# Seven products of quadrants instead of eight in the down projections of two squared-relu MLPs

## The chip, the cores and the metric

The kernel runs on one core of a Trainium2 chip. The metric is the device time of one execution in microseconds (us). The inputs are float32; 512 tokens, 1024 features.

## The reference, cut to what matters

A first block (attention mixers, gated MLP, embedding gate) is followed by two layers; each ends with a squared-relu MLP, between two RMS norms and with a residual:

```python
def squared_relu_mlp(h, w_up, w_down):        # h 512x1024, w_up 1024x4096, w_down 4096x1024
    u = jax.nn.relu(h @ w_up)
    return (u * u) @ w_down

        ff = squared_relu_mlp(rms_norm(h, mlp_norm_pre[layer]), mlp_w_up[layer], mlp_w_down[layer])
        h = h + rms_norm(ff, mlp_norm_post[layer])
```

## The kernel before

All activations lie feature-major: a tile holds 128 features (partitions) by 512 tokens. A product in float32 precision is made of three passes: each operand is split into a rounded high part (`hi`, a cast on ScalarE) and the rest (`lo`, a subtraction on VectorE), and `mm3` (line 404 for each matmul) adds hi·hi, hi·lo and lo·hi in PSUM. Weights come by DMA as 128x1024 tiles (`raw`, four buffers), and are split in `_split` into `whi` (L361, ScalarE) and `wlo` (L365, VectorE), four buffers each. `take` hands out one weight tile; it issues the splits up to three tiles ahead and the loads up to five tiles ahead, in the order that a dry run has recorded. Activations are split in `split_to` (L562 on ScalarE, L563 on VectorE).

The engines run their own queues. The framework that builds the program puts in the semaphores and lays out the order within each queue; the order of the source is its priority.

The working tiles of 128x512 float32 (2 KB a partition) come from 72 slots, taken and given back by `get` and `put`, oldest free first. PSUM has eight banks of 128x512, from `ps` and `pput`.

One MLP (`mlp`): `layer_start` computes the first five up tiles (four of them in two token halves) and the statistics of the norm. Each of 32 up tiles is 8 k tiles x 3 passes = 24 matmuls with the weights stationary and the 512 tokens moving. Its output gets a relu on VectorE (L1902), a Square on ScalarE (L1907) and the split. After 16 up tiles `half_down` multiplies them with the first K half of the down weights: 8 output tiles, each 16 k x 3 matmuls, copied to `ya` by ScalarE (L1585). After the other 16, `close` does the second K half: six output tiles whole, the last two (`tail = 2`) in two token halves of 256 columns, so that the norm (`rms_g`: column sums by matmul, a reciprocal root in small VectorE operations in `rsqrt`, a broadcast by two transposes, L588) and the residual (`postnorm`) of one token half run under the matmuls of the other. The second half's norm and residual (`fin`) run under the first matmuls of the next layer, or at the end of the kernel, where POOL and VectorE share the additions and the result is stored (L636).

After the first MLP, `xs` (the residual stream, 8 tiles) stays in its slots; `spill` and `fill`, which write it to DRAM and read it back, are used around the mixers only.

The value projections (`vals`) are token-major: there the activations are the stationary operand and 256 columns of weights move.

Of the kernel before, what the change touches and what calls it, by code (L numbers as in the profile page):

```python
# [19 lines left out]
P = 128  # L20
T = 512
# [1 line left out]
NT = T // P  # L23
EPS = 1e-6
BIGM = 1e30
NSLOT = 72
LOOK_SPLIT = 3
LOOK_DMA = 5
LO_CHUNK = 1024
# [32 lines left out]
NCOL = _n  # L62
NPAIR = 22
UP_ORDER = [m for i in range(NPAIR) for m in (i, i + NPAIR)]


def _bucket(rel):
# [56 lines left out]
    return np.ascontiguousarray(a.reshape(k // (nk * P), P, nk * n))  # L124


def _cv(v):
    return np.asarray(v).reshape(-1, P).T

# [6 lines left out]
def layout(I):  # L136
    I = {k: np.asarray(v) for k, v in I.items()}
    A = {}
    A["xt"] = np.ascontiguousarray(I["x"][0].T).reshape(8, P, T)
    A["pt"] = np.ascontiguousarray(I["p"][0, 0].T).reshape(2, P, T)  # L140
    A["pos"] = np.ascontiguousarray(I["positions"][0].reshape(NT, P).T)
    w = I["w_in"][0]
    sl = lambda a, n: w[:, a:a + n]
    q0, kv0, g0, cq0, ckv0, kr0, mg0 = 0, 512, 1280, 1304, 1560, 1688, 1720
    kv = [sl(kv0 + 128 * i, 128) for i in range(6)]
    A["win"] = _mtiles(np.concatenate(
        [kv[0], kv[1], kv[2], kv[4], sl(q0, 512), sl(cq0, 256), sl(ckv0, 128), sl(mg0, 2048)], 1))
# [24 lines left out]
    A["kvv"] = np.concatenate([_ktiles(wkv[:, 1024 + 256 * i:1280 + 256 * i], 4) for i in range(4)], 0)  # L172
    A["wq"] = _mtiles(I["b_w_q_2"][0])
    A["bwo"] = _mtiles(I["b_w_out_2"][0])
    for l in range(2):
        A[f"mup{l}"] = _mtiles(I["mlp_w_up_2"][l])
        A[f"mdn{l}"] = _mtiles(I["mlp_w_down_2"][l])
# [90 lines left out]
class Em:  # L268
    def __init__(self, nc, pools, A, order=None, dbg=None):
        self.nc, self.pools, self.A = nc, pools, A  # L270
        self.order, self.rec = order, []
        self.dry = order is None
        self.pos = self.dma_pos = self.spl_pos = 0
        self.raw, self.ready = {}, {}
        self.free = deque(range(NSLOT))
# [5 lines left out]
        self.fin = None  # L281
        self.closing = False
        self.peak = 0
        self.dbg = dbg or {}


    def get(self, name, dt=F32):
        i = self.free.popleft()
        self.peak = max(self.peak, NSLOT - len(self.free))
        if self.dry:  # L290
            t = _Null()
        else:
            t = self.pools["slots"].tile([P, T], dt, name=name, tag=f"sl{i}", bufs=1)
        self.slot_of[id(t)] = (i, t)
        return t

    def put(self, *ts):
        for t in ts:
            i, _ = self.slot_of.pop(id(t))
            self.free.append(i)  # L300

    def tile(self, pool, shape, dt, name, bufs=None):
        if self.dry:
# [22 lines left out]

    @staticmethod
    def width(key):
        return key[2] * key[4] * P if key[0] == "A" else key[3]

    def _dma(self, i):
        key = self.order[i]
        e = self.width(key)
        t = self.tile("raw", [P, 1024], F32, "raw")
        if key[0] == "A":
# [61 lines left out]
    def takeT(self, w, i, nk, n):  # L397
        hi, lo = self.take(("T", w, i, nk * n))
        f = lambda t: t.rearrange("p (k c) -> p k c", k=nk)
        return f(hi), f(lo)  # L400


# [311 lines left out]
    def finish(self, gen=()):  # L714


        for n, _ in enumerate(gen):
            if n + 1 in FIN and self.fin is not None:
                if next(self.fin, self) is self:
                    self.fin = None  # L720
        if self.fin is not None:
            drain(self.fin)
            self.fin = None

    @contextmanager
    def after(self, *ins):
# [140 lines left out]

def _emit(s):
    nc = s.nc
    V, S, G = nc.vector, nc.scalar, nc.gpsimd  # L870
    A = s.A

# [1002 lines left out]
    ho = [ho[i] for i in range(8)]  # L1875
    for i, (h, l) in enumerate(ho):
        s.dump("ho", h.bitcast(F32) if not s.dry else h, i)
    fill(xs)
    s.wlo = LO_ENG[3]
    ys, ss = [], s.get("ss")  # L1880
    (acts,) = s.close("awo", ho, 0, 4, s.yevac(ss, ys, "a_post"), ss, ys, xs, ["mlp_pre0"], pre)


    def mlp(l, acts, gains):


        first, banks, eps = layer_start(f"mup{l}", acts, True)
        yacc = []
        ss = s.get("ss")
        for half in range(2):  # L1890
            hid = []
            for m in range(16 * half, 16 * half + 16):
                if m < 5:
                    pieces = first[m]
                    ps = pieces[0][0]
# [12 lines left out]
                hid.append(s.split(t))  # L1908
                s.put(t)
            if half == 0:  # L1910
                half_down(f"mdn{l}", hid, 0, yacc)
        s.putacts(acts)
        return s.close(f"mdn{l}", hid, 16, 2, acc_evac(ss, yacc, f"mlp_post{l}"), ss, yacc, xs, gains, None, eps,
                       s.out if l else None)

    (qacts,) = mlp(0, acts, ["b_pre"])

# [167 lines left out]
    do = [do[i] for i in range(8)]  # L2085
    for i, (h, l) in enumerate(do):
        s.dump("do", h.bitcast(F32) if not s.dry else h, i)
    fill(xs)
    s.wlo = LO_ENG[5]
    ys, ss = [], s.get("ss")  # L2090
# [6 lines left out]
def tile_kernel(ctx, tc, A, out, dbg=None):  # L2097
# [15 lines left out]
    e2.out = out  # L2113
    e2.tc = tc
    _emit(e2)
# [14 lines left out]
```

## Time and profile before

| | |
|---|---|
| median of 3 runs | 2155.44 us (2153.95 to 2160.1) |
| the profiled execution | 2165.75 us, its span 2164.0 us |
| granted TensorE clock over the span | 0.984 |
| TensorE (PE) busy | 2118.6 us, 11650 matmuls |
| VectorE (DVE) busy | 1385.8 us, 2934 instructions |
| ScalarE (ACT) busy | 1041.9 us, 1966 instructions |
| moved by DMA | 222.58 MB, mean 103 GB/s |

The span goes from the first to the last instruction. The time of the execution lies a little above the span. PEld is TensorE's weight load, SPq the queue that issues the DMAs. The end of a matmul is modelled, since matmuls are pipelined; the distance from start to start tells what one costs.

### The profile page before, as it was taken

What the parts mean: (1) busy time and instruction counts of PE and PEld (TensorE: products, weight loads), DVE (VectorE), ACT (ScalarE), POOL (GpSimd) and SP (SyncE); (2) the same over time, 40 slices, a digit from 0 to 9 for tenths busy, and PEclk for the clock granted to TensorE, in tenths of its full rate; (3) what the DMA queues carried; (4) which work ended last, traced back from release to release, by engine and by line L of the source; (5) the groups of instructions that cost most, each with busy time, mean ns of one, the idle gap of its engine ahead of it and who ended that gap; (6) DMA issues with size and microseconds to landing.
All of it is one profiled execution on the core that took longest, in us unless ns stands there. A gap on an engine that the chain in (4) does not pass through costs nothing.

```text
span 2164.0 us, 30979 instructions
## 1 busy us (share of the span) xinstructions
PE 2118.6 (98%) x11650; PEld 1814.9 (84%) x11650; DVE 1385.8 (64%) x2934; ACT 1041.9 (48%) x1966; POOL 143.8 (7%) x264
## 2 busy tenths in 40 slices
PE   9999999999999999899999999999999999999997
PEld 8888877988888899789779888888988889888887
DVE  7686688787367578877997632444777758423443
ACT  5565576554344455555655432333456645323341
POOL 0000002000000000422430000000000000000001
PEclk9999999999999999899999999999999989999999
DMA  6113256332333333122121333224463531332331
GB/s 220 43 62 101 66 171 216 98 107 77 104 103 98 106 112 127 54 75 69 59 93 65 107 98 98 97 92 133 136 188 103 147 102 60 97 98 98 98 97 40
DMA packets 95125, 222.58 MB, mean 103 GB/s; under 512 B 9696, under 2 KB 32080, under 8 KB 94976
## 3 DMA queue, kind: packets, MB, share of 16 engines
q1 hardware_dynamic: 94976, 220.61, 32.1%
q8 instruction: 91, 1.49, 0.3%
q14 instruction: 58, 0.48, 0.1%
HBM read 198.25 MB, written 17.87 MB: 100 GB/s over the span
## 4 chain that ended last, share of the span: by engine, by line
PE 49%; DVE 4%; POOL 2%; issue 1%; ACT 1%; DMA 1%; POOLq 0%; SPq 0%; ACTq 0%; DVEq 0%
PE ps L404 47%; PE s L404 1%; PE o L404 1%; POOL lx L1759 1%; POOL lx L1758 1%; DMA dtab<-rexp 1%; PE rms L404 1%; DVE wlo L365 0%; DVE lx L1761 0%; PE rms L588 0%; DVE lx L1762 0%; DMA raw<-in_mup 0%; DVE sc L1787 0%; DVE ls L1669 0%; PE pt L829 0%
## 5 line engine op out<-in xcount | busy, mean ns | idle before, releaser
L404 PE MATMUL ps<-ah,whi 128*128 128x512 f32 (+1 forms) x2414 | 916.0, 380 | 1.7 <-ACT whi L361 1.1
L404 PE MATMUL ps<-ah,wlo 128*128 128x512 f32 (+1 forms) x2414 | 904.6, 375 | 0.0
L404 PE MATMUL ps<-al,whi 128*128 128x512 f32 (+1 forms) x2414 | 900.4, 373 | 1.9 <-DVE al L566 1.4
L361 ACT CAST whi<-raw 128x1024 fp32r<-128x1024 f32 (+4 forms) x323 | 316.4, 983 | 572.6 <-PE ps L404 545.3
L365 DVE TENSOR_TENSOR wlo<-raw,whi 128x1024 fp32r<-128x1024 f32 (+4 forms) x323 | 374.2, 1160 | 266.2 <-ACT whi L361 264.2
L404 PEld LDWEIGHTS ps<-ah,wlo 128*128 128x128 f32 x2414 | 454.3, 188 | 86.7
L404 PEld LDWEIGHTS ps<-al,whi 128*128 128x128 f32 x2414 | 455.0, 188 | 83.1 <-DVE al L566 2.3
L404 PEld LDWEIGHTS ps<-ah,whi 128*128 128x128 f32 x2414 | 455.2, 189 | 78.2 <-ACT whi L361 1.4
L1902 DVE TENSOR_SCALAR mu<-ps 128x512 f32<-128x512 f32 (+1 forms) x72 | 45.2, 632 | 149.6 <-PE ps L404 149.6
L404 PE MATMUL ps<-ah,wh 128*128 128x256 f32 x428 | 122.2, 285 | 0.0
L404 PE MATMUL ps<-al,wh 128*128 128x256 f32 x428 | 121.0, 283 | 0.0
L404 PE MATMUL ps<-ah,wl 128*128 128x256 f32 x428 | 121.0, 283 | 0.0
L797 ACT ACTIVATE p<-p,am 128x128 f32<-128x128 f32 (+3 forms) x160 | 88.5, 554 | 39.6 <-DVE am L795 38.6
L404 PE MATMUL ps<-whi,ah 128*128 128x256 f32 (+2 forms) x300 | 88.8, 296 | 3.9 <-DVE am L795 3.3
L404 PE MATMUL ps<-wlo,ah 128*128 128x256 f32 (+2 forms) x300 | 87.2, 291 | 0.9 <-DVE wlo L365 0.9
L621 DVE TENSOR_TENSOR ss<-ss,sq 128x512 f32<-128x512 f32 (+1 forms) x117 | 67.3, 575 | 31.5 <-ACT sq L620 30.5
L404 PE MATMUL ps<-whi,al 128*128 128x256 f32 (+2 forms) x300 | 87.1, 291 | 0.0
L404 PEld LDWEIGHTS ps<-al,wh 128*128 128x128 f32 x428 | 81.9, 191 | 0.3
L404 PEld LDWEIGHTS ps<-ah,wh 128*128 128x128 f32 x428 | 81.9, 191 | 0.2
L404 PEld LDWEIGHTS ps<-ah,wl 128*128 128x128 f32 x428 | 81.9, 191 | 0.0
L565 ACT ACTIVATE ah<-x,cols 128x256 fp32r<-128x256 f32 (+1 forms) x96 | 49.5, 540 | 52.8 <-DVE x L632 49.6
L835 ACT CAST pth<-pt 128x128 fp32r<-128x128 f32 (+3 forms) x128 | 49.9, 431 | 40.7 <-PE pt L829 38.3
(326 smaller groups left out, 2740.6 us busy)
## 6 DMA issues: line engine op xcount, KB each, us to landing
raw<-in_mup SPq DMA_DIRECT2D x64, 512.0 KB, 3.5
raw<-in_mdn SPq DMA_DIRECT2D x64, 512.0 KB, 3.8
raw<-in_up SPq DMA_DIRECT2D x44, 512.0 KB, 3.5
raw<-in_win SPq DMA_DIRECT2D x26, 512.0 KB, 3.9
raw<-in_awin SPq DMA_DIRECT2D x24, 512.0 KB, 3.5
thd<-th SPq DMA_DIRECT2D x24, 256.0 KB, 2.3
th<-thd SPq DMA_DIRECT2D x24, 256.0 KB, 4.3
raw<-in_down SPq DMA_DIRECT2D x16, 384.0 KB, 3.1
```

Of the source, the lines that this page charges most:

```text
L361: self.whi_ins = self.nc.scalar.copy(hi[:, :e], raw[:, :e])
L365: eng.tensor_tensor(lo[:, d], raw[:, d], hi[:, d], op=ALU.subtract)
L404: self.nc.tensor.matmul(ps, l, r, start=first, stop=last, skip_group_check=skip)
L565: self.hi_ins = nc.scalar.activation(hi, src, AF.Copy, scale=scale)
L621: nc.vector.tensor_tensor(ss[:, c], ss[:, c], t[:, c], op=ALU.add)
L797: nc.scalar.activation(d, d, AF.Exp, scale=-1.0, bias=m[:, qb:qb + 1], accum_out=sm[:, qb:qb + 1])
L835: nc.scalar.copy(h[:, z:z + n], pt[:, 0:n])
L1758: G.tensor_tensor(x4[1], v5(b4[:, :, 1, :]), v5(mid), op=ALU.subtract)
L1759: G.tensor_tensor(x4[0], v5(mid), v5(b4[:, :, 0, :]), op=ALU.subtract)
L1902: V.tensor_scalar(t[:, c], ps, 0.0, None, op0=ALU.max)
```

## The change

The hidden activations A (512 tokens x 4096) and the down weights B (4096 x 1024) are cut into quadrants: token halves, K halves and output halves. Seven products of sums of quadrants give the four output quadrants (Winograd's form of Strassen's scheme) where eight products of plain quadrants did before. The output quadrants are token-major, 128 tokens by 512 features: activations are stationary, 512 columns of weights move.

The up tiles are reordered so that a tile of the first K half is followed by its partner of the second. Four chunks of 8 up tiles (four pairs) are each followed by `seven`: products 1, 7, 6, 4, 5, 2, 3, each over 4 k tiles x 2 token blocks x 3 passes, in PSUM banks X, Y and Z (two each). Products that belong together accumulate in the same bank, and `add` adds a bank's state to the tile C of an output quadrant (a copy on ScalarE the first time); Z holds product 2 over all chunks. `combine` makes the sums of weight quadrants on VectorE, in place, in tiles that are kept (`b11`, `b12`, `t`, two buffers each); the second use of quadrants B21 and B22 is loaded anew. The relu moves to ScalarE. The norm's sums come from Squares with an accumulator, `back` transposes the scaled result to feature-major on TensorE and adds it to the residual. The 12 highest slots are given up while an MLP runs (`high`) for the kept quadrants, and `xs` is spilled and filled in each MLP.

```diff
@@ _dma, new combine, _split
+        if key[0] == "S":
+            _, w, g, r = key
+            a = self.A[w][g]
+            for q, name in {1: ((0, "b11"),), 7: ((1, "b12"), (3, None)), 4: ((2, None),), 2: ((2, None),),
+                            3: ((3, None),)}.get(r, ()):
+                if name is None:
+                    t = self.raw[i] = self.tile("raw", [P, 1024], F32, "raw")
+                else:
+                    t = self.kept[name, g] = self.tile("quad", [P, 1024], F32, name, 2)
+                self.nc.sync.dma_start(t, a[q])
+            return
...
+    def combine(self, i):
+        _, w, g, r = self.order[i]
+        sub = lambda o, a, b, op=ALU.subtract: self.nc.vector.tensor_tensor(o, a, b, op=op)
+        if r in (2, 3):
+            return self.raw.pop(i)
+        if r == 1:
+            return self.kept["b11", g]
+        if r == 5:
+            t = self.kept.pop(("b12", g))
+            sub(t, t, self.kept.pop(("b11", g)))
+            return t
+        if r == 7:
+            t = self.kept["t", g] = self.tile("quad", [P, 1024], F32, "t", 2)
+            sub(t, self.raw.pop(i), self.kept["b12", g])
+        elif r == 6:
+            t = self.kept["t", g]
+            sub(t, t, self.kept["b11", g], ALU.add)
+        else:
+            t = self.kept.pop(("t", g))
+            sub(t, self.raw.pop(i), t)
+        return t
...
-        raw = self.raw.pop(i)
+        raw = self.combine(i) if self.order[i][0] == "S" else self.raw.pop(i)
@@ new seven
+        def product(r, pss, first, stop):
+            for g in (2 * ch, 2 * ch + 1):
+                hi, lo = s.takeS(w, g, r)
+                for k in range(2):
+                    h, l = ops[r].pop(2 * g + k)
+                    for tb in range(2):
+                        c = slice(tb * P, tb * P + P)
...
+                        s.mm(pss[tb], h[:, c], hi[:, k, :], f, False, True)
+                        s.mm(pss[tb], h[:, c], lo[:, k, :], False, False, True)
+                        s.mm(pss[tb], l[:, c], hi[:, k, :], False, e, True)
+                    yield
...
+        X, Y = [s.ps(), s.ps()], [s.ps(), s.ps()]
+        drain(product(1, X, True, True))
+        add(1, 1, X)
+        drain(product(7, Y, True, True))
+        add(2, 2, Y)
+        drain(product(6, X, False, True))
+        add(2, 1, X)
+        drain(product(4, Y, False, True))
+        add(2, 1, Y)
+        s.pput(*Y)
+        drain(product(5, X, False, True))
+        add(2, 2, X)
+        between(0)
...
+        drain(product(2, Z, ch == 0, last))
...
+        for n, _ in enumerate(product(3, X, False, True)):
+            if n == 2:
+                between(2)
+        add(1, 2, X)
...
@@ mlp
+        s.high("quad")
         first, banks, eps = layer_start(f"mup{l}", acts, True)
...
+        spill(xs)
...
+        def back(i):
+            c = slice(0, 256) if i == 2 else slice(256, 512)
+            for f in range(0, 8, 2):
+                ps = s.ps()
+                for k in range(2):
+                    for tb in range(2):
+                        o = 256 * k + P * tb
+                        d = (f + k) % 4 * P
+                        nc.tensor.transpose(ps[:, o:o + P], C[i, 1 + f // 4, tb][:, d:d + P], s.ident)
+                for k in range(2):
+                    x = xs[f + k][:, c]
+                    V.scalar_tensor_tensor(x, ps[:, 256 * k:256 * k + 256], s.col(f"mlp_post{l}", f + k), x,
+                                           op0=ALU.mult, op1=ALU.add)
...
-                    V.tensor_scalar(t[:, c], ps, 0.0, None, op0=ALU.max)
+                    S.activation(t[:, c], ps, AF.Relu)
...
+                    s.split_to(q[:, lo], q[:, up], t1[:, up])
...
+                    V.tensor_tensor(u1[:, lo], t1[:, up], t1[:, lo], op=ALU.subtract)
+                else:
+                    V.tensor_tensor(u1[:, up], t1[:, lo], t[:, lo], op=ALU.add)
+                    V.tensor_tensor(u2[:, lo], u1[:, up], t1[:, up], op=ALU.subtract)
+                    V.tensor_tensor(u2[:, up], t[:, up], u2[:, lo], op=ALU.subtract)
...
+                    for src, r0, r1, rl in ((u1, 7, 5, 5), (u2, 6, 3, 3), (t, 4, 2, 2)):
+                        h, lw = s.split(src)
...
-            if half == 0:
-                half_down(f"mdn{l}", hid, 0, yacc)
...
+            if last:
+                s.putacts(acts)
+                fill(xs)
+            seven(f"mdn{l}", ch, ops, C, Z, last, ending if last else lambda n: None)
+        s.high("high")
```

## Rows read from the trace of the kernel before

**Rows 1.** The page, its head and part 1: busy us of each engine.

```profile
span 2164.0 us, 30979 instructions
...
PE 2118.6 (98%) x11650; PEld 1814.9 (84%) x11650; DVE 1385.8 (64%) x2934; ACT 1041.9 (48%) x1966; POOL 143.8 (7%) x264
```

**Rows 2.** The chain that ended last, first MLP: start, length, what, count.

```profile
1200.87 279.14 PE ps L404 x1219
```

**Rows 3.** Windows of the first MLP: busy us and instructions, clock, DMA, GB/s.

```profile
1264.00:1352.00 88.00, 88.00 (x386) 72.22 (x385) 20.99 (x18) 21.48 (x26) 0.00 (x0) 1.00 0.30 96
1352.00:1440.00 88.00, 88.00 (x386) 72.22 (x385) 39.84 (x47) 34.80 (x48) 0.00 (x0) 1.00 0.30 96
```

**Rows 4.** Timeline of TensorE, first and last of 20 matmuls of 256 columns.

```profile
2141.05 0.28 PE L404 MATMUL ps<-al,wh 128*128 128x256 f32 x1
...
2143.33 0.28 PE L404 MATMUL ps<-ah,wl 128*128 128x256 f32 x1
```

**Rows 5.** The end of the kernel: the chain that ended last, and SP's stores.

```profile
2140.04 0.59 PE rms L404 x4
2140.64 2.97 PE ps L404 x24
2143.61 0.22 PE rms L588 x2
2143.83 7.20 PE ps L404 x60
2151.03 0.02 issue
...
2153.07 0.17 DVE rv L582
...
2153.27 0.17 DVE ry L603
...
2155.04 0.17 DVE ry L610
...
2157.68 3.84 SPq L636 DMA_DIRECT2D out<-x  x8
```

**Rows 6.** Transposes on TensorE's timeline, and the window around them.

```profile
1615.55 1.69 PE L829 MATMUL pt<-ident,p 128*128 128x128 f32 x14
1617.00 0.48 PE L404 MATMUL ps<-ah,whi 128*128 128x512 f32 x1
...
1612.00:1620.00 8.00, 8.00 (x55) 6.92 (x53) 4.12 (x8) 5.83 (x14) 0.62 (x3) 1.00 0.37 132
```

**Rows 7.** Timeline, first and last of 17 matmuls of the value projection.

```profile
1612.15 0.28 PE L404 MATMUL ps<-wlo,ah 128*128 128x256 f32 x1
...
1614.03 0.28 PE L404 MATMUL ps<-whi,al 128*128 128x256 f32 x1
```

**Rows 8.** Timeline of VectorE without gaps, where starts tell the price.

```profile
1190.87 1.23 DVE L365 TENSOR_TENSOR wlo<-raw,whi 128x1024 fp32r<-128x1024 f32 x1
1192.00 0.69 DVE L621 TENSOR_TENSOR ss<-ss,sq 128x512 f32<-128x512 f32 x1
1192.60 0.42 DVE L1902 TENSOR_SCALAR mu<-ps 128x256 f32<-128x256 f32 x1
1192.94 0.69 DVE L621 TENSOR_TENSOR ss<-ss,sq 128x512 f32<-128x512 f32 x1
```

**Rows 9.** Groups, 1186 to 1480 us: busy us, mean ns, idle before, releaser.

```profile
L365 DVE TENSOR_TENSOR wlo<-raw,whi 128x1024 fp32r<-128x1024 f32 x55 | 67.5, 1228 | 86.7 <-ACT whi L361 86.7
L361 ACT CAST whi<-raw 128x1024 fp32r<-128x1024 f32 x55 | 57.9, 1053 | 184.5 <-PE ps L404 184.5
...
L1907 ACT ACTIVATE mu<-mu 128x512 f32<-128x512 f32 x32 | 20.0, 629 | 0.1
L562 ACT CAST ah<-mu 128x512 fp32r<-128x512 f32 x32 | 19.7, 621 | 0.9
L1902 DVE TENSOR_SCALAR mu<-ps 128x512 f32<-128x512 f32 x28 | 19.4, 692 | 74.8 <-PE ps L404 74.8
...
L1585 ACT COPY ya<-ps 128x512 f32<-128x512 f32 x8 | 4.6, 577 | 0.0
```

**Rows 10.** Timeline of ScalarE and VectorE at the end of one up tile.

```profile
1252.99 1.05 ACT L361 CAST whi<-raw 128x1024 fp32r<-128x1024 f32 x1 [3.25 <-PE ps L404]
...
1253.22 0.69 DVE L1902 TENSOR_SCALAR mu<-ps 128x512 f32<-128x512 f32 x1 [2.76 <-PE ps L404]
...
1253.95 0.63 ACT L1907 ACTIVATE mu<-mu 128x512 f32<-128x512 f32 x1
1254.08 1.23 DVE L365 TENSOR_TENSOR wlo<-raw,whi 128x1024 fp32r<-128x1024 f32 x1 [0.16 <-ACT whi L361]
...
1254.61 0.62 ACT L562 CAST ah<-mu 128x512 fp32r<-128x512 f32 x1
...
1255.27 0.69 DVE L563 TENSOR_TENSOR al<-mu,ah 128x512 fp32r<-128x512 f32 x1
```

**Rows 11.** DMA issues (KB each, us to landing), and the busiest DMA window.

```profile
raw<-in_mdn SPq DMA_DIRECT2D x64, 512.0 KB, 3.8
...
1570.00:1580.00 10.00, 9.45 (x42) 7.27 (x40) 9.43 (x14) 4.47 (x6) 0.00 (x0) 1.00 0.98 308
```

**Rows 12.** Groups of the whole span: the read of an accumulator on ScalarE.

```profile
L797 ACT ACTIVATION_READ_ACCUMULATOR p<-p,am 128x1 f32 x160 | 30.0, 188 | 0.0
```

**Rows 13.** Window of `layer_start` in the first MLP.

```profile
1181.00:1203.00 22.00, 22.00 (x175) 21.12 (x174) 21.95 (x48) 15.20 (x26) 0.00 (x0) 1.00 0.28 95
```

More of the change, by code (lines that the diff above doesn't have):

```diff
@@ L25 @@
 BIGM = 1e30
-NSLOT = 72
+NSLOT, NLOW = 72, 60
 LOOK_SPLIT = 3
@@ L64 @@
 UP_ORDER = [m for i in range(NPAIR) for m in (i, i + NPAIR)]
+MLP_ORDER = [m for i in range(16) for m in (i, i + 16)]
 def _bucket(rel):
@@ L281, in __init__ @@
         self.fin = None
+        self.fin_at = FIN
         self.closing = False
+        self.low = False
+        self.kept = {}
         self.peak = 0
@@ L287, in get @@
     def get(self, name, dt=F32):
-        i = self.free.popleft()
+        if self.low:
+            i = next(i for i in self.free if i < NLOW)
+            self.free.remove(i)
+        else:
+            i = self.free.popleft()
         self.peak = max(self.peak, NSLOT - len(self.free))
@@ L292, in get @@
         else:
-            t = self.pools["slots"].tile([P, T], dt, name=name, tag=f"sl{i}", bufs=1)
+            t = self.pools["slots" if i < NLOW else "high"].tile([P, T], dt, name=name, tag=f"sl{i}", bufs=1)
         self.slot_of[id(t)] = (i, t)
@@ L300, in put, with high @@
             self.free.append(i)
+    def high(self, name):
+        if name == "high":
+            self.free.extend(range(NLOW, NSLOT))
+        elif self.high_is == "high":
+            for i in range(NLOW, NSLOT):
+                self.free.remove(i)
+        self.high_is = name
+        self.low = name != "high"
+        if self.dry:
+            return
+        if self.high_pool is not None:
+            self.high_pool.__exit__(None, None, None)
+        self.high_pool = self.tc.tile_pool(name=f"{name}{len(self.rec)}{self.pos}", bufs=1)
+        self.pools[name] = self.high_pool.__enter__()
     def tile(self, pool, shape, dt, name, bufs=None):
@@ L717, in finish @@
         for n, _ in enumerate(gen):
-            if n + 1 in FIN and self.fin is not None:
+            if n + 1 in self.fin_at and self.fin is not None:
                 if next(self.fin, self) is self:
@@ L723, in finish @@
             self.fin = None
+        self.fin_at = FIN
     @contextmanager
@@ L1877, in _emit @@
         s.dump("ho", h.bitcast(F32) if not s.dry else h, i)
+    s.low = True
     fill(xs)
@@ L1881, in _emit, with seven, add @@
     (acts,) = s.close("awo", ho, 0, 4, s.yevac(ss, ys, "a_post"), ss, ys, xs, ["mlp_pre0"], pre)
+    def seven(w, ch, ops, C, Z, last, between):
+        def product(r, pss, first, stop):
[5 more added lines that the diff above has]
+                        c = slice(tb * P, tb * P + P)
+                        f, e = first and g % 2 + k == 0, stop and g % 2 + k == 2
+                        s.mm(pss[tb], h[:, c], hi[:, k, :], f, False, True)
+                        s.mm(pss[tb], h[:, c], lo[:, k, :], False, False, True)
+                        s.mm(pss[tb], l[:, c], hi[:, k, :], False, e, True)
+                    yield
+            for t in ops.get(("put", r), ()):
+                s.put(t)
+            ops.pop(("put", r), None)
+        def add(i, j, pss):
+            for tb in range(2):
+                if (i, j, tb) in C:
+                    V.tensor_tensor(C[i, j, tb], C[i, j, tb], pss[tb], op=ALU.add)
+                else:
+                    t = C[i, j, tb] = s.get("C")
+                    S.copy(t, pss[tb])
+        X, Y = [s.ps(), s.ps()], [s.ps(), s.ps()]
[11 more added lines that the diff above has]
+        between(0)
+        if not Z:
+            Z += [s.ps(), s.ps()]
+        drain(product(2, Z, ch == 0, last))
+        if last:
+            add(1, 1, Z)
+            s.pput(*Z)
+            between(1)
+        for n, _ in enumerate(product(3, X, False, True)):
+            if n == 2:
+                between(2)
+        add(1, 2, X)
+        s.pput(*X)
+        between(3)
@@ L1884, in mlp, with squares @@
     def mlp(l, acts, gains):
+        s.high("quad")
         first, banks, eps = layer_start(f"mup{l}", acts, True)
[L1888 to L1892, printed above, removed]
+        spill(xs)
+        C, Z = {}, []
+        sums, outs = {}, [[] for _ in gains]
+        def squares(i, j):
+            if i not in sums:
+                sums[i] = s.small("hs", 4)
+            t = s.get("sq")
+            for tb in range(2):
+                S.activation(t, C[i, j, tb], AF.Square, accum_out=sums[i][:, 2 * tb + j - 1:2 * tb + j])
+            s.put(t)
@@ new lines, in scale @@
+        def scale(i):
+            h2 = sums[i].rearrange("p (a j) -> p a j", a=2)
+            v = s.small("rv", 2)
+            V.tensor_tensor(v, h2[:, :, 0], h2[:, :, 1], op=ALU.add)
+            t0 = 0 if i == 2 else 2
+            V.scalar_tensor_tensor(v, v, 1.0 / D, eps[:, t0:t0 + 2], op0=ALU.mult, op1=ALU.add)
+            r = s.rsqrt(v, 2)
+            for tb in range(2):
+                S.activation(C[i, 1, tb], C[i, 1, tb], AF.Copy, scale=r[:, tb:tb + 1])
+                V.tensor_scalar(C[i, 2, tb], C[i, 2, tb], r[:, tb:tb + 1], None, op0=ALU.mult)
@@ new lines, in back @@
+        def back(i):
[3 more added lines that the diff above has]
+                for k in range(2):
+                    for tb in range(2):
+                        o = 256 * k + P * tb
[5 more added lines that the diff above has]
+                                           op0=ALU.mult, op1=ALU.add)
+                    if l:
+                        nc.sync.dma_start(s.out[f + k][:, c], x)
+                    for g, o in zip(gains, outs):
+                        if len(o) <= f + k:
+                            o.append((s.get("ah", F32R), s.get("al", F32R)))
+                        s.split_to(o[f + k][0][:, c], o[f + k][1][:, c], x, s.col(g, f + k))
+                s.pput(ps)
+            s.put(*[C.pop((i, j, tb)) for j in (1, 2) for tb in range(2)])
@@ L1893, in mlp, with ending @@
+        def ending(n):
+            if n == 0:
+                squares(2, 1)
+                squares(2, 2)
+                scale(2)
+            elif n == 1:
+                squares(1, 1)
+            elif n == 2:
+                back(2)
+            else:
+                squares(1, 2)
+                scale(1)
+        for ch in range(4):
+            ops = {r: {} for r in range(1, 8)}
+            last = ch == 3
+            for m in range(8 * ch, 8 * ch + 8):
                 if m < 5:
@@ L1907, in mlp, with fin @@
                 S.activation(t, t, AF.Square)
[L1908 to L1914 removed]
+                p = m // 2
+                lo, up = slice(0, 256), slice(256, 512)
+                if m % 2 == 0:
+                    t1 = t
+                    q = s.get("qh", F32R)
+                    s.split_to(q[:, lo], q[:, up], t1[:, up])
+                    ops[1][p] = q[:, lo], q[:, up]
+                    u1, u2 = s.get("u1"), s.get("u2")
+                    V.tensor_tensor(u1[:, lo], t1[:, up], t1[:, lo], op=ALU.subtract)
+                else:
+                    V.tensor_tensor(u1[:, up], t1[:, lo], t[:, lo], op=ALU.add)
+                    V.tensor_tensor(u2[:, lo], u1[:, up], t1[:, up], op=ALU.subtract)
+                    V.tensor_tensor(u2[:, up], t[:, up], u2[:, lo], op=ALU.subtract)
+                    s.put(t1)
+                    puts = [(1, (q,))]
+                    for src, r0, r1, rl in ((u1, 7, 5, 5), (u2, 6, 3, 3), (t, 4, 2, 2)):
+                        h, lw = s.split(src)
+                        s.put(src)
+                        ops[r0][p], ops[r1][p] = (h[:, lo], lw[:, lo]), (h[:, up], lw[:, up])
+                        puts.append((rl, (h, lw)))
+                    for r, ts in puts:
+                        ops.setdefault(("put", r), []).extend(ts)
+            if last:
+                s.putacts(acts)
+                fill(xs)
+            seven(f"mdn{l}", ch, ops, C, Z, last, ending if last else lambda n: None)
+        s.high("high")
+        def fin():
+            yield
+            back(1)
+        s.fin, s.fin_at = fin(), (2, 6)
+        return outs
     (qacts,) = mlp(0, acts, ["b_pre"])
@@ L2087, in _emit @@
         s.dump("do", h.bitcast(F32) if not s.dry else h, i)
+    s.low = True
     fill(xs)
```

20 lines of the change are left out of this document (16 added, 4 removed).

## The prediction

> **What bounds the kernel now.** I read the page first. TensorE is busy for 98% of the span, VectorE for 64%, ScalarE for 48% [rows 1]. A busy TensorE can hide waits, since its ends are modelled, so I went on to the chain of work that ended last, over the stretch of the first MLP. There it is one piece: 1219 matmuls into `ps` in 279.14 us, with no other engine in it [rows 2]. That is 0.229 us for one matmul of 512 columns, from start to start. The windows over the same MLP agree: TensorE busy throughout, clock 1.00, VectorE busy 21 of 88 us under the first half of the down projection and 39.8 of 88 under the second half of the up projection [rows 3]. So in both MLPs the time is the number and width of the matmuls, until something else becomes late.
>
> **What is removed.** Before, one down projection has 8 output tiles in two K halves. The first half is 8 x 16 x 3 = 384 matmuls of 512 columns, the second has 6 x 16 x 3 = 288 of them and, for the last two tiles, two token halves: 2 x 2 x 16 x 3 = 192 of 256 columns. After, seven products of 16 k tiles x 2 token blocks x 3 passes are 672 matmuls of 512 columns. So 672 stay 672, and what goes are the 192 narrow ones. Nineteen steps of such matmuls take 2.28 us [rows 4], 0.120 us each: 192 x 0.120 = 23.0 us for each MLP. The norm's matmuls go too: 0.59 us for the column sums and 0.22 us for the broadcast, for each token half [rows 5]. That is 1.6 us in the first MLP and 0.8 us in the second, whose other half lies in the tail.
>
> **What TensorE gets.** 32 transposes of 128x128 for each MLP. Fourteen such transposes hold TensorE from 1615.55 to 1617.00 us, 0.104 us each; the norm's two take 0.11 each [rows 6, 5]. I take 0.11: 3.5 us in the first MLP; in the second 16 are in the stream, 1.8 us, and 16 in the tail. The Trainium skill (TensorE: Matmul & The Clock Gate, Part 4: PE-mode transpose) gives about 275 ns for one in a kernel, which agrees with the modelled duration of the row but not with its starts; by that figure the 64 would be an estimated 17.6 us instead of 7.0, and the sum below 10.6 us worse.
>
> The operands change sides: activations become the stationary operand, weights the moving one. The value projections already run so, at 256 columns: 16 steps in 1.88 us, 0.118 each [rows 7], against 0.120 the other way round. So I keep 0.229 for 512 columns; the bound below is no change, the bound above is that 512-wide ones are slower than any row shows, which I price at nothing for want of a reason.
>
> Sum on TensorE: first MLP -23.0 - 1.6 + 3.5 = -21.1 us; second -23.0 - 0.8 + 1.8 = -22.0 us; together -43.1 us.
>
> **The tail of the second MLP.** Before: from the last matmul into `ps` at 2151.03 to the end of the span, 13.0 us, of which 1.94 us is the reciprocal root (2153.27 to 2155.21) and eight output stores occupy SP for 3.84 us [rows 5]. After: two additions from PSUM (2 x 0.69), a Square (0.63 [rows 9]) with the read of its accumulator (0.19 [rows 12]), two small operations (0.17 each and the hand-over between engines) and the root (1.9) end at 4.4; two scalings to 5.6; four transposes and their latency to 6.2; then eight updates, whose stores leave at 0.5 us each, to 10.6; and the 2.5 us that lie between the last store's end (2161.52) and the end now. That is 13.1 us: no change, 1 us either way.
>
> **What VectorE and ScalarE get.** The new layout works through a chunk of 8 up tiles, then seven products of 168 matmuls: 8 x 24 x 0.229 = 44.0 us and 168 x 0.229 = 38.5 us on TensorE. Back to back, VectorE starts a 1024-wide subtraction 1.13 us before its next instruction, a 512-wide one 0.60, a 256-wide one 0.34 [rows 8]; from PSUM I take the whole 0.69 [rows 9]. A chunk then needs 22 low parts of weights (24.9), 8 sums of weight quadrants (9.0), 12 additions of products (8.3; in the first chunk eight are copies on ScalarE) and for each of four pairs five 256-wide and three 512-wide operations (3.5, so 14.0): 56 of 82.5 us. ScalarE: 22 casts at 1.05, 16 relu and Square at 0.63, four pairs at 2.3 [rows 9]: 42 us. On average both fit.
>
> The tight place is the start of the products. A weight buffer holds four, so the cast for a step waits until the step four before has left TensorE (ScalarE's 184.5 us idle before the cast, all released by `ps` [rows 9]). One step is 12 matmuls, 2.75 us. Up to the fifth product, 22.0 us in, VectorE owes six low parts (6.8), six quadrant sums (6.8), three pairs of additions (4.1) and the rest of the last activations (2.8): 20.5 of 22.0 us. It fits only if VectorE doesn't stand still while ScalarE casts. Between a quadrant sum and its low part lies a cast of 1.05 us, so the order in VectorE's queue decides. The trace shows that order: in the source the activation's split (L562, L563) comes before the next weight tile's (L361, L365), yet on ScalarE the cast of weights goes first, and on VectorE L365 starts at 1254.08 and L563 at 1255.27 [rows 10]. Queues are thus laid out by what is ready. Then the sums for products 7 and 5, which need only loaded quadrants, move into the up tiles, where VectorE needs some 20 of 44 us, and the tight stretch falls to about 18 of 22 us.
>
> I take 0.6 us for each of eight chunks and 1 us where each MLP joins the next work: 7 us. Both ends are kept for the range: nothing, and the source's order below.
>
> **Loads.** A chunk has 20 loads of 512 KB where 16 had the same time: 10.5 MB in 82.5 us, 127 GB/s, against 96 now; a load lands 3.8 us after issue, and one window moves 308 GB/s [rows 3, 11]. Cover is the buffers: four raw, two of each kept quadrant. `xs` is spilled and filled (16 x 256 KB), needed only tens of us later. I cost loads at nothing; without cover it is 3.8 us for each chunk, 30 us. Moving the relu to ScalarE (0.58 us for a copy of that width from PSUM, against 0.69 on VectorE [rows 9]) costs nothing, as ScalarE has 40 us left in a chunk.
>
> Sum: -43.1 + 7 = -36 us. The profiled execution takes 2165.75 us (span 2164.0), 10 us above the median of 2155.44; taken from the median this is 2119 us, a profiled span near 2128.
>
> **The rivals.**
> 1. TensorE keeps pace, 0 to 18 us lost in both MLPs: 2112 to 2130. For it: VectorE's 68% and the order by readiness. Chance 0.58.
> 2. VectorE is late by 2 to 4 us in each chunk, because the layout doesn't pull the sums forward, or because the first chunk meets a VectorE that is busy for 21.95 of 22 us just before it now [rows 13]: 16 to 35 us lost, about 2137. Chance 0.19.
> 3. VectorE becomes the bound of the products: its queue keeps the source's order. Each of the combined steps then takes 1.13 + 1.1 + 1.13 = 3.4 us instead of 2.75, and the additions wait behind them. Followed step by step, the fourth product may first overwrite its bank at 21.5 us instead of 16.5, the fifth at 29.5 instead of 22.0, and the chunk ends at 46.4 instead of 38.5 us: 7.9 us, for eight chunks 63 us, so +20 and about 2177, slower. It decides from 5.4 us for a chunk (43.1 / 8). The Trainium skill (Perfetto Trace Analysis, Tensor Engine Instruction) says that VectorE and ScalarE are strict FIFO; the trace agrees in so far as VectorE stands idle 86.7 us before L365 in this MLP, released by the cast [rows 9]. Against it: rows 10. Chance 0.11.
> 4. Transposes lower the clock: all 64 at half rate are 7 us more, and 96 matmuls of the next layer behind them at half rate 11.5 us: 2137. The same section of the Trainium skill says that transposes don't count as work for the clock. Against it: a window with 18 of them has clock 1.00 [rows 6]. Chance 0.03.
> 5. Weights land late: 30 us, 2149. Chance 0.05.
> 6. The narrow matmuls go, but weights as 512-wide moving operand run slower, by 3% or more over 1344 matmuls (9 us and up): 2128 to 2165. Chance 0.04.
>
> **How the numbers follow.** A measurement of this kernel can tell 0.3%, 6.5 us, from no change. Faster: 0.58 + 0.19 + 0.03 and most of 5 and 6, 0.84. Same: what lies between 2149 and 2162, 0.05. Slower: rival 3, 0.11. The likeliest case's own range is 2110 to 2130. For 8 in 10 the range goes from 2108 (nothing lost and a tail 1 us better, with the spread of the runs) to 2152 (rivals 2, 4 and 5); left out are rival 3 and the ends of 6.
>
> **What would show it.** Right: the chain still one piece of `ps` through both MLPs, 192 narrow matmuls fewer and 32 transposes more in each, `wlo` finished before its step, VectorE near 68% in a chunk. Wrong: idle on TensorE's row before `ps`, released by VectorE's `wlo` or by the additions from PSUM, repeating in every chunk (rival 3 if about 8 us, 2 if less); starts of 512-wide matmuls more than 0.229 us apart (6); `in_mdn` as releaser (5); a clock under 1.00 behind the transposes (4).

## The result, and the profile after

After: 2120.85 us, the median of 4 runs (2120.62 to 2124.78); before: 2154.69 us in 4 runs. The ratio is 0.9846, its 95% interval 0.9821 to 0.9872. Forecast were 2119 us and a range of 2108 to 2152.

The profiled execution took 2120.62 us (2165.75 before). The page's head and busy times, against [rows 1]:

```profile
span 2118.8 us, 30910 instructions
...
PE 2075.4 (98%) x11306; PEld 1761.0 (83%) x11306; DVE 1570.2 (74%) x3192; ACT 1148.0 (54%) x2142; POOL 138.2 (7%) x256
```

344 matmul instructions fewer (384 narrow ones and 24 of the norms gone, 64 transposes new), VectorE 184 us busier, and TensorE still busy for 98%. Line 477 is now the line of each matmul (404 before). The chain that ended last, in the first MLP and then in the second, against [rows 2]:

```profile
1195.92 304.12 PE ps L477 x1308
...
1793.27 308.31 PE ps L477 x1326
```

In each MLP it is one piece of matmuls from the first up tiles into the last chunk's products: nothing waits. But 304.12 / 1308 is 0.2325 us for a matmul, and [rows 2] give 0.2290. Two windows, the up tiles of chunk 1 (chunks are counted from 0) and its seven products, against [rows 3]:

```profile
1254.00:1298.00 44.00, 44.00 (x190) 35.61 (x190) 27.18 (x39) 24.01 (x37) 0.00 (x0) 1.00 0.29 97
1298.00:1338.00 40.00, 40.00 (x173) 32.26 (x172) 28.99 (x34) 17.40 (x19) 0.00 (x0) 1.00 0.47 158
```

VectorE is busy for 56.2 of 84 us; the forecast's budget was 56 of 82.5. The clock is 1.00 in both.

To see where time went, I cut the span where the norm's eight column sums of a layer's start run on TensorE (from 1199.9 us in the first MLP before, from 1194.9 us after). Us of each stretch:

```
                 MLP 0 (to wq's)   wq's to MLP 1's   MLP 1 (to the end)
before               356.8              264.5              342.8
after                341.4              256.0              326.6
difference           -15.4               -8.5              -16.2
```

The MLPs give 31.6 us and the medians 33.8. The two profiles differ by 45, so most of the 13.5 us outside the MLPs doesn't come back in the medians; the last experiment looks at where it lies.

### The profile page after: what moved, and what is told of

Read it like the earlier page. It is cut to its first block, busy times and chain, and to the rows that moved or that the text cites. A ratio compares the mean times of both kernels' runs of the same rounds, so it can differ in the third digit from the quotient of the medians.

```text
span 2118.8 us, 30910 instructions
## 1 busy us (share of the span) xinstructions
PE 2075.4 (98%) x11306; PEld 1761.0 (83%) x11306; DVE 1570.2 (74%) x3192; ACT 1148.0 (54%) x2142; POOL 138.2 (7%) x256
## 4 chain that ended last, share of the span: by engine, by line
PE 47%; DVE 5%; POOL 2%; issue 1%; ACT 1%; DMA 1%; SPq 0%; DVEq 0%; POOLq 0%; ACTq 0%
PE ps L477 45%; POOL lx L1834 1%; DMA dtab<-rexp 1%; POOL lx L1833 1%; DVE wlo L433 1%; PE o L477 1%; PE s L477 1%; PE rms L477 0%; DVE x L2057 0%; DVE lx L1836 0%; DVE p L869 0%; DVE lx L1837 0%; DVE p L2236 0%; DMA raw<-in_mup 0%; DVE rt L682 0%
## 5 line engine op out<-in xcount | busy, mean ns | idle before, releaser
L477 PE MATMUL ps<-ah,whi 128*128 128x512 f32 (+1 forms) x1966 | 737.3, 376 | 0.6 <-ACT ah L638 0.3
L477 PE MATMUL ps<-al,whi 128*128 128x512 f32 (+1 forms) x1966 | 728.1, 370 | 1.9 <-DVE al L639 1.4
L477 PE MATMUL ps<-ah,wlo 128*128 128x512 f32 (+1 forms) x1966 | 728.4, 371 | 0.0
L433 DVE TENSOR_TENSOR wlo<-raw,whi 128x1024 fp32r<-128x1024 f32 (+5 forms) x299 | 343.7, 1151 | 177.7 <-ACT whi L429 175.6
L429 ACT CAST whi<-raw 128x1024 fp32r<-128x1024 f32 (+5 forms) x299 | 290.7, 976 | 338.4 <-PE ps L477 314.1
L477 PE MATMUL ps<-whi,ah 128*128 128x512 f32 (+2 forms) x684 | 240.2, 351 | 3.6 <-DVE am L869 3.0
L477 PE MATMUL ps<-wlo,ah 128*128 128x512 f32 (+2 forms) x684 | 238.5, 349 | 0.9 <-DVE wlo L433 0.9
L477 PE MATMUL ps<-whi,al 128*128 128x512 f32 (+2 forms) x684 | 238.3, 349 | 0.0
L477 PEld LDWEIGHTS ps<-whi,ah 128*128 128x128 f32 x684 | 130.0, 190 | 22.2 <-DVE am L869 3.2
L477 PEld LDWEIGHTS ps<-wlo,ah 128*128 128x128 f32 x684 | 130.1, 190 | 19.1 <-DVE wlo L433 1.2
## 6 DMA issues: line engine op xcount, KB each, us to landing
xsp<-x SPq DMA_DIRECT2D x32, 256.0 KB, 2.5
x<-xsp SPq DMA_DIRECT2D x32, 256.0 KB, 2.8
```

The lines of the kernel that those rows point to most:

```text
L429: self.whi_ins = self.nc.scalar.copy(hi[:, :e], raw[:, :e])
L433: eng.tensor_tensor(lo[:, d], raw[:, d], hi[:, d], op=ALU.subtract)
L477: self.nc.tensor.matmul(ps, l, r, start=first, stop=last, skip_group_check=skip)
```

## The experiments

Each was profiled, and those with an interval were also timed against the kernel before on the same chip. The stretches are those above.

**One MLP alone.** The second MLP keeps its old code and weight layout.

```diff
...
-    mlp(1, acts, [])
+    mlp_old(1, acts, [])
```

> Only the first MLP has the seven products; the second is computed as before. Theory (each MLP gains by its own narrow matmuls, and what was gained elsewhere in the two profiles belongs to the executions, not to the change): the stretch from the first MLP's statistics to those of wq takes 341.5 us as after, the stretch from the second MLP's statistics to the end 342.7 us as before, and the ratio to the kernel before is half way, 0.992 (some 2137 us). Rival (the change also gains by what it does to the slots and spills around the MLPs, or the MLPs gain only together): a ratio at or under 0.988, or at or over 0.997.

Measured: 341.4 us and 342.8 us, each to 0.1 us what the theory says. The ratio is 0.9938 (0.9915 to 0.9962), median 2143.89 us, 7 us above the expected 2137. Its runs spread from 2135.8 to 2145.8 us; in the profiled one the span is 20.7 us over that of after, 16.2 of them in the second MLP and 4.5 outside both. The interval holds the 0.992 and leaves out both numbers of the rival. Each MLP's gain is its own.

**Eight products.**

```diff
...
-        drain(product(2, Z, ch == 0, last))
+        W = [s.ps(), s.ps()]
+        drain(product(2, Z, ch == 0, last, W))
+        s.pput(*W)
```

> Product 2 is computed a second time, with the same weights and activations, into two banks that nobody reads: eight products' matmuls, nothing more for VectorE, ScalarE or the loads. Theory (the time of the products is the number of their matmuls): 24 more in each of 8 chunks, 192 x 0.2333 = 44.8 us, so about 2166 us, ratio 1.005. Rival (part of the products' time is waiting for VectorE, hidden in longer spacings): the new matmuls fill such waits, and the time rises by 30 us or less, ratio under 0.999.

Measured: the MLPs take 363.3 and 349.0 us, 21.9 + 22.4 = 44.3 us more than after (44.8 expected); ratio 1.0059 (1.0038 to 1.008), 2168.39 us. With eight products' matmuls the layout is no longer faster than before: its time is the number of its matmuls.

**VectorE in the order of the source.** Each VectorE instruction of the chunk loop is issued after the one ahead of it in the source.

```diff
...
+                with self.tc.issue_after(self.last.ins):
+                    r = f(*a, **k)
...
+        V.on, V.last = True, None
         for ch in range(4):
```

> VectorE's instructions are held in the order of the source within the loop over chunks; they are the same instructions. My third rival said that this order costs 7.9 us for each of eight chunks, 63 us: 2184 us, ratio 1.013. Theory (the order by readiness is what let TensorE keep pace): at least 16 us, the lower end of rival 2 (ratio 0.992 or more), up to these 63. Rival (VectorE had room in any order): under 6 us, ratio under 0.988.

Measured: 2184.88 us, ratio 1.0141 (1.0113 to 1.0169): 64 us above the kernel after, where rival 3 said 63. The MLPs give 32.3 + 24.8 = 57.1 of them. From the first product's first matmul to the start of the seventh product's last one takes 46.3 us in chunks 1 and 2 of the first MLP (39.0 after); the forecast had 46.4 for the chunk. Chunk 0, whose additions are mostly copies on ScalarE, takes only 42.7. The waits of TensorE in the first MLP (us in total, times, longest; line 505 is the matmul, line 292 the helper that holds VectorE's order), and then the chain in chunk 1's products:

```profile
PE ps L505 <- DVE C L292: 13.4, 9, 1.6
PE ps L505 <- DVE wlo L292: 5.1, 11, 0.5
PE ps L505 <- DVE x L292: 4.8, 2, 3.2
```

```profile
1319.49 1.06 ACT whi L457
1320.58 1.22 DVE wlo L292
1321.80 1.15 DVE t L292
1323.03 1.06 ACT whi L457
1324.11 1.23 DVE wlo L292
1325.33 1.20 DVE C L292 x2
```

A sum of quadrants (`t`), a cast, a low part: 3.5 us for a step in which TensorE works 2.8, and the additions into `C`, which free a product's banks, stand behind them. The third wait, for updates of the residual (`x`), lies at the join with the next layer. Behind it the granted clock fell: it is 1.00 in the 10 us from 1530 and 0.66 in the 10 from 1540, where the longer of these waits (3.2 us) ends and 256-wide matmuls start 0.213 us apart; after, the same join runs at 1.00. A third of 10 us, an estimated 3.4 of the first MLP's 32.3 us, is this slower clock.

```profile
1530.00:1540.00 10.00, 6.83 (x35) 4.18 (x33) 9.96 (x15) 5.95 (x11) 0.00 (x0) 1.00 0.58 188
1540.00:1550.00 10.00, 7.78 (x46) 7.54 (x47) 6.76 (x17) 3.47 (x7) 0.00 (x0) 0.66 0.87 294
```

**Only the weights in that order.** The chain holds the sums and low parts alone.

```diff
-        sub = lambda o, a, b, op=ALU.subtract: self.nc.vector.tensor_tensor(o, a, b, op=op)
+        sub = lambda o, a, b, op=ALU.subtract: self.wv.tensor_tensor(o, a, b, op=op)
...
-        eng = self.nc.gpsimd if where == "g" or (where == "a" and i % 2) else self.nc.vector
+        eng = self.nc.gpsimd if where == "g" or (where == "a" and i % 2) else self.wv
```

> The kernel after, with only VectorE's work on weights (sums of quadrants and low parts) held in the order of the source among itself; activations and the additions of products stay free to go by readiness. So the sums can still be pulled ahead of activations, not ahead of low parts of earlier weight tiles. Theory (what let TensorE keep pace is that a sum isn't queued behind the low part of the step before, which waits for a cast): a good part of the 57 to 64 us of the full source order, 16 us or more, ratio 0.992 or above. Rival (it is the order of the weights against activations and additions that counts): under 6 us, ratio under 0.9875.

Measured: 2134.27 us, ratio 0.991 (0.9895 to 0.9925), which is 13.4 us above the kernel after; in the MLPs only 4.1 + 3.4 = 7.5. Neither side's number came: a small part, but not nothing.

**Weights and additions in that order.**

```diff
-                    V.tensor_tensor(C[i, j, tb], C[i, j, tb], pss[tb], op=ALU.add)
+                    (V if s.dry else s.wv).tensor_tensor(C[i, j, tb], C[i, j, tb], pss[tb], op=ALU.add)
```

> As the run that held the weights' sums and low parts in the order of the source, and now the additions of finished products (from PSUM into the accumulators) with them in one chain; only the work on activations stays free to go by readiness. Theory (in the full source order it is the additions, queued behind low parts that wait for casts, that make TensorE wait for its banks): most of that order's 57 us in the MLPs comes back, 40 us or more over the kernel after, ratio 1.003 or above; TensorE waits for the additions. Rival (the rest of the 57 us comes from activations that hold the weights up): no more than the 7.5 us that the weights' own order cost in the MLPs, ratio 0.99.

Measured: 2148.11 us, ratio 0.9966 (0.9955 to 0.9977); in the MLPs 14.6 + 8.5 = 23.1 us. Both sides miss again. Of the 57.1 us the weights' own order makes 7.5, the additions queued with them 15.6 more, and the remaining 34.0 come only when the work on activations is held as well. In this run too the clock falls at the join behind the first MLP (0.73 and 0.92 in the 20 us from 1520), as it does in the full source order and not with the weights alone: some 3.5 us of the 15.6, an estimate from these two windows, are that. No single queue neighbour is the cause.

**The relu back on VectorE.**

```diff
-                    S.activation(t[:, c], ps, AF.Relu)
+                    V.tensor_scalar(t[:, c], ps, 0.0, None, op0=ALU.max)
```

> The kernel after, with the relu back on VectorE: 16 x 0.69 = 11 us more for VectorE in the up tiles of each chunk, 67 of 82.5 us. Theory (up tiles have room: VectorE needs some 20 of 44 us there): 0 to 4 us, ratio 0.985. Rival (the move of the relu is what makes room for the sums pulled ahead): over 10 us, ratio 0.989 or more.

Measured: 341.3 and 326.5 us in the MLPs, as after; ratio 0.9845 (0.9807 to 0.9884). My 16 x 0.69 counted twice what was moved: a chunk has 8 up tiles, so 8 x 0.69 = 5.5 us (VectorE's busy time rises by 36.5 us over the eight chunks). VectorE has room for 5.5 us more per chunk in the order by readiness; 11 us were not tried.

**One bank for each product.** Now the spacing.

```diff
...
-                        s.mm(pss[tb], h[:, c], hi[:, k, :], f, False, True)
...
+                        s.mm(pss[0], h[:, c], hi[:, k, :], f, False, True)
...
```

> Both token blocks of a product are accumulated into one PSUM bank, and both additions read that bank (so the two token blocks of a product are summed): the same matmuls, but without a change of bank after every three. Theory (the change of bank makes 512-wide matmuls start 0.2333 us apart instead of 0.2289): all 1344 matmuls of an MLP go back to 0.2289, some 4.9 us for each MLP, ratio 0.980 against 0.9846. Rival (the swap of operands, weights moving and activations stationary, does it): spacing 0.2333 in the products as after, ratio 0.9846.

Measured: ratio 0.9852 (0.983 to 0.9874); 341.1 and 326.6 us. The chain inside the first chunk's products, in the kernel after and then in this one:

```profile
1215.96 34.07 PE ps L477 x146
```

```profile
1219.84 34.30 PE ps L477 x147
```

0.2333 us for a matmul in both (34.07 / 146, 34.30 / 147). The change of bank isn't it.

**VectorE relieved.**

```diff
...
+        if self.order[i][0] == "S":
...
+            self.ready[i] = (hi[:, :e], hi[:, :e])
+            return
```

> The kernel after, without VectorE's work on the down weights: no sums of quadrants (each product takes one loaded quadrant) and no low parts (the cast stands in for them), so 14 low parts and 8 sums of 22 and 8 go from each chunk. The matmuls are the same in number, size and operands' sides. Theory (spacing belongs to the operands' sides): the products still start every 0.2333 us and the two MLPs take what they took after, within 2 us. Rival (VectorE's accesses slow the matmuls): 0.2289, some 10 us less in both MLPs.

Measured, a window and the chain in the first chunk's products:

```profile
1228.00:1268.00 40.00, 40.00 (x173) 32.16 (x172) 9.67 (x11) 18.09 (x22) 0.00 (x0) 1.00 0.51 162
```

```profile
1227.87 30.33 PE ps L480 x130
```

VectorE is busy for 9.7 of 40 us instead of 29.0, and the matmuls still start 0.2333 us apart (30.33 / 130). The MLPs take 341.3 and 326.5 us. VectorE's accesses aren't it either.

**The operands swapped, and nothing else.**

```diff
...
+                        s.mm3(ps, (h[:, c], l[:, c]), (hi[:, d], lo[:, d]), a + k == 0, a + k == 15)
```

> The kernel before, with one thing changed: in the first half of each squared-relu MLP's down projection the operands change sides (a 128x128 piece of an activation is stationary, 512 columns of the weight tile move). The same loads, casts, number of matmuls, one PSUM bank for each output tile; what it adds up is no longer the down projection. Theory (the swap by itself makes 512-wide matmuls start 0.2333 us apart): these 384 matmuls of each MLP take 89.6 us instead of 87.9. Rival (the wider spacing comes from something else of the new layout, such as VectorE's and ScalarE's work beside it): 0.2289 as before.

Measured, three pieces of the chain: up tiles ahead of the swapped stretch, the swapped stretch, and up tiles behind it.

```profile
1209.99 40.06 PE ps L404 x175
...
1263.80 40.37 PE ps L404 x173
...
1359.94 40.13 PE ps L404 x172
```

0.2289, 0.2333 and 0.2333 us: the swap widens the spacing by 2%, and the 512-wide matmuls behind it, whose operands are not swapped, keep it until the next layer. The MLPs take 361.5 and 347.5 us, 4.7 us each more than before, although the swapped matmuls alone account for 384 x 0.0044 = 1.7; with the 672 behind them it is 4.6.

**Narrow work between.**

```diff
+    def kick():
+        ps = s.ps()
+        for o in range(0, T, P):
+            nc.tensor.transpose(ps[:, o:o + P], s.ident, s.ident)
+        s.pput(ps)
...
+            kick()
```

> The kernel after, with four 128x128 transposes of the identity into an unread bank ahead of each product and of the up tiles of chunks 1 to 3: 31 x 4 transposes for each MLP at 0.09 to 0.11 us, 11 to 14 us for each MLP, some 25 us in all. Theory (with activations stationary and weights moving 512-wide matmuls start 0.2333 us apart of themselves, and the up tiles of chunks 1 and 3 only carry that spacing on until something narrow comes between): products 0.2333 as after, up tiles of all chunks 0.2289. Rival (the spacing is a state that the start of the products happens to enter, and narrow work leaves it anywhere): 0.2289 in products too. Second rival (the wider spacing in the up tiles has another cause, and narrow work does nothing): chunks 1 and 3 stay at 0.2333.

Measured: ratio 0.9978 (0.9965 to 0.9991), 2150.39 us; the MLPs are 11.7 + 12.2 = 23.9 us longer than after. The chain, from the sixth product to the up tiles of chunk 1:

```profile
1249.38 0.44 PE ps L1963 x4
1249.82 5.60 PE ps L477 x24
1255.42 0.43 PE ps L1963 x4
1255.85 5.64 PE ps L477 x24
1261.49 0.44 PE ps L1963 x4
1261.93 43.28 PE ps L477 x189
```

Products stay at 5.60 / 24 = 0.2333 us, while the up tiles behind the transposes are back at 43.28 / 189 = 0.2290. After, the same up tiles ran at 40.37 / 173 = 0.2333:

```profile
1255.86 40.37 PE ps L477 x173
```

So the products have the wider spacing of themselves, and only what follows can be freed. The price of freeing it (0.44 us) eats half of what it gives in 192 matmuls (0.84). Transposes ahead of the up tiles of chunks 1 and 3 alone would give an estimated 1.6 us in both MLPs, less than the runs differ among themselves; that was not tried.

**Before, once more.** The same code.

> The kernel before, unchanged, profiled once more. Theory (the 8.6 us that the first two profiles differ in between the two MLPs are clock stretches of one execution): here that stretch is under 262 us instead of 264.5, and a window under clock 0.8 at 1740 to 1760 us is gone. Rival (the change gains there): 264 to 265 us again. The MLPs take 356.8 and 342.7 us by both.

Measured: 356.8, 263.3 and 342.8 us, in an execution of 2161.08 us. My theory missed: the stretch between the MLPs stays long, and the window under a low clock is there again. The profile before and this one:

```profile
1740.00:1760.00 20.00, 18.35 (x73) 14.84 (x72) 12.75 (x52) 8.32 (x22) 0.00 (x0) 0.68 0.37 127
```

```profile
1740.00:1760.00 20.00, 18.45 (x71) 15.28 (x70) 10.90 (x39) 6.39 (x13) 0.00 (x0) 0.66 0.26 79
```

In every other run that stretch takes 252.8 to 259.7 us. Over the whole stretch the granted clock is 0.96 and 0.97 in the two profiles of before and 1.00 after. The shortest stretch is that of the swapped kernel, which differs from before in the MLPs alone and has no window under 1.00 there; at a clock of 1.00 throughout, the kernel after (256.0 us) and the one with one bank for each product (255.5) are no shorter than it. So the 8.5 us go with the granted clock in attention, whose code is the same in all kernels. Whether the change makes such dips rarer, or two of two profiles of before just have one, stays open. Both executions of before lie over its median. By the medians 33.8 - 31.6 = 2.2 us come from outside the MLPs, which is less than the interval of the ratio leaves open (5.5 us either way), so no gain there is shown.

## Why the prediction was right

The mechanism was right: narrow matmuls go, nothing waits, and queues laid out by readiness let VectorE keep pace. That the time came within 2 us is luck in part, because two misses met: 7 us of stalls that didn't come, and 11 us that I had priced at nothing. In the MLPs alone 31.6 us came where the forecast had 36. Term by term, for both MLPs:

- **Narrow matmuls, -46.0 forecast:** start to start the 256-wide ones sum to 45.6 us in the first MLP before and 22.9 after, -22.8; with -23.2 in the second, -46.0 in all. Right.
- **Transposes, +5.3 forecast:** 5.2, that is 3.5 us for the 32 in the first MLP, 1.7 us for the 16 in the second's stream, 0.104 to 0.109 each, and a window over 16 of them (1518 to 1530 us) has clock 1.00. So rival 4 fell. The 275 ns of the Trainium skill (TensorE: Matmul & The Clock Gate, Part 4: PE-mode transpose, where the sentence in rival 4 stands too) don't show as occupied time here.
- **Wide matmuls at 0.229, priced at nothing:** this is the step that failed. I took the rows of 256 columns [rows 4, 7], 0.120 and 0.118 us, to mean that the swap costs nothing, and carried that over to 512 columns, where it costs 0.0044 us. One pair of rows could not show that: in the trace before, 256-wide matmuls with the weights stationary start 0.113 us apart in one stretch (14.17 / 125) and 0.120 in another (10.08 / 84, both below). Summed start to start it is +4.9 us in the first MLP and +4.8 in the second, 9.7 us. It is rival 6's mechanism, at 2% instead of the 3% from which I counted it, and it includes up tiles that only inherit it.

```profile
1181.93 14.17 PE ps L404 x125
1506.94 10.08 PE ps L404 x84
```

- **Stalls, +7:** none. The chain is one piece in both MLPs, and the only wait of TensorE on its list for the first MLP is 0.3 us, for an accumulator ahead of a transpose.
- **The norm's matmuls, -2.4:** start to start they give -1.0 in the first MLP and -0.5 in the second's stream; I had priced them by lengths on the chain.
- **The tail, 0:** +1.2. From the end of the last matmul to the end of the span 14.1 us (13.0 before). The chain of the end, against [rows 5] (line 1984 adds a product, 2031 squares, 683 is in the root, 2054 transposes, 2057 updates the residual):

```profile
2103.24 2.04 DVE x L2057 x5
2105.28 0.60 DVE C L1984
...
2105.91 0.73 ACT sq L2031 x2
2106.64 0.02 issue
2106.66 0.73 ACT sq L2031 x2
...
2109.58 0.17 DVE ry L683
...
2110.41 1.67 PE ps L2054 x6
2112.08 0.02 issue
2112.10 2.44 DVE x L2057 x6
```

The last matmul ends at 2104.73. The root ends 5.0 us later instead of 4.4: I had left out the 0.5 us until the first addition starts, in which VectorE is still busy with the updates of the first token half (the first line). The updates begin 7.4 us after that matmul instead of 6.2, behind transposes that come after 5.7 us of idle TensorE: the granted clock is 0.50 there, the lower level (2110 to 2114 us), and they start 0.213 us apart, twice the price. From there the updates and their stores take 4.3 us (4.4 priced) and the rest 2.5 (2.5).

Together: -46.0 + 5.2 + 9.7 - 1.5 + 1.2 = -31.4 us, against the -31.6 measured. The forecast's -36 was -43.1 + 7.

The reading on which the forecast chose between its rivals, that queues are laid out by what is ready and the quadrant sums move into the up tiles, is shown. VectorE's timeline after, in the up tiles of chunk 1, whose products start at 1299.1 (line 392 is `sub` in `combine`):

```profile
1265.58 1.23 DVE L392 TENSOR_TENSOR t<-raw,b 128x1024 f32<-128x1024 f32 x1 [2.60 <-DMA raw<-in_mdn]
...
1268.19 1.22 DVE L392 TENSOR_TENSOR b<-b,b 128x1024 f32<-128x1024 f32 x1
...
1271.20 1.22 DVE L392 TENSOR_TENSOR t<-raw,b 128x1024 f32<-128x1024 f32 x1
...
1274.75 1.22 DVE L392 TENSOR_TENSOR b<-b,b 128x1024 f32<-128x1024 f32 x1
```

The sums for products 7 and 5 run 24 to 34 us ahead of the products. In the order of the source the first of them starts at 1302.36, 2.9 us before its chunk's products (1305.24). Rival 3 was therefore right about its mechanism, and near in its sum (57 us in the MLPs of 63), though not as eight equal shares: 3.8 us in the first chunk of each MLP, 7.3 to 8.6 in the others, and the rest at the joins with the slower clock there. It was wrong that this kernel's queue has that order. Held in the order of the source, the same instructions cost 57 us in the MLPs. The strict FIFO of the Trainium skill (Perfetto Trace Analysis, Tensor Engine Instruction) agrees with that.

Rival 2 (16 to 35 us) fell with the stalls. Rival 5 did too: nothing on TensorE waits for a load, and loads for the products land in 3.3 us.

## What to carry to other kernels

Where TensorE's chain is one unbroken piece, count its matmuls: the narrow matmuls and the transposes, counts of instructions times a start-to-start row, held to 0.1 us, while the norm's, priced by lengths on the chain, missed by 0.9. A price taken at one width is not a price at another, and one pair of rows is no comparison where the trace has several spacings for one form: if the change runs an operand arrangement at a width that no row shows, keep a few per cent for it in the sum, not in a rival. When a change adds work to an engine with room, ask first in which order its queue is laid out: here the same VectorE instructions cost nothing in one order and 57 us in another, while 5.5 us more work for VectorE per chunk cost nothing.

## What the hardware showed that I had not expected

- 512-wide matmuls start at one of two spacings, 0.2289 or 0.2333 us, both at clock 1.00 and without a wait. With a 128x128 piece of the activations stationary and 512 columns of weights moving it was 0.2333 in every product looked at, whatever bank they wrote and however idle VectorE was.
- The wider spacing outlasts its cause. With the first half of the down projection swapped, the unswapped matmuls behind it kept 0.2333 us; four 128x128 transposes ended it.
- Without such transposes the kernel after leaves it in the up tiles of chunk 2 (38.23 / 167 = 0.2289 us in the chain) but not in those of chunks 1 and 3, in both MLPs. TensorE doesn't wait ahead of them. Waits in the products change where it is left, but by no rule that I found. With only the weights in the order of the source, TensorE waits in the products of the first MLP's chunk 2, and the up tiles of chunk 3 behind them are at 38.22 / 167 = 0.2289. With the additions held too, it waits in the products of the second MLP's chunk 1, and the up tiles of chunk 2 behind them stay at 0.2333 (the last line). What ends it, and what in the chip makes the two spacings, no run here shows.

```profile
1341.91 38.23 PE ps L477 x167
...
1431.88 38.22 PE ps L497 x167
...
1963.90 38.27 PE ps L497 x164
```
